# Rates, decays, operands, pairs and keys of each half of the heads pinned behind single steps of the column GEMMs, key copies on ACT

## The chip, the cores and the metric

The kernel runs on one core of a Trainium2 chip. The metric is the device time of one execution in microseconds (us).

## The reference

Two layers, each a half-step SwiGLU FFN, two token mixers side by side, and another half-step FFN; 256 tokens of 1024 numbers, all in fp32. The part around the change is the second mixer, RWKV-7:

```
p_b = token_shift_mix(p[..., GATE_WIDTH + 2 * A_WIDTH:], mu)      # p = h @ w_in
r, k, v = p[..., :B_WIDTH], p[..., B_WIDTH:2*B_WIDTH], p[..., 2*B_WIDTH:3*B_WIDTH]
log_w = -softplus(-(w0 + tanh(w_down) @ w2)) - 0.5
decay = exp(-exp(log_w))
a = sigmoid(a0 + a_down @ a2)
if v_first is not None:                                            # layer 1 only
    v = v + (v_first - v) * sigmoid(v0 + v_res_down @ v2)
kk = heads(k * k_k)
kk = kk / maximum(sqrt(sum(kk * kk, axis=-1)), 1e-12)
k = k * (1 + (a - 1) * k_a)
def step(state, inp):                                              # over the tokens
    sa = einsum('bhvk,bhk->bhv', state, kk_t)
    state = state * w_t - sa * (kk_t * a_t) + v_t * k_t
    return state, einsum('bhvk,bhk->bhv', state, r_t)
```

The first mixer (gMLP) needs `u` and `v` columns of the same `p`, a layer norm and a causal 128x128 product.

## The kernel before

**The GEMMs.** All large products run in fp32r with a high and a low part of each operand, three matmuls for one (`mm3` and the three lines of `chunk_b`). Weights come by DMA from SP's queue in units of 512 KB; each unit is cast on ACT (L220, high part) and subtracted on DVE (L221, low part), four units ahead of their use. ACT and DVE thus have a standing duty per unit beside whatever else they do.

**The columns of the second mixer.** k, r and v of each half of the heads (g = 0, 1; four column blocks of 128 each) are chunks of 96 matmuls of 128x256 (`chunk_b`), four steps of 24, one weight unit each. Behind a chunk `shift` mixes each block with the token before it: ACT L533, then DVE L534.

**What is made of them, per half g.** `rwkv_rates`: squares of k on ACT (L630), head sums on PE (L633), their inverse roots on DVE and POOL (L636, L637), spread on ACT (L642); the LoRA products of decay and a (L648, L661) with tanh on ACT (L650, L663) and one DVE pass (L651); in layer 1 also the mix of v with the first layer's (L674). `rwkv_pairs`, per pair of blocks q = 0, 1: cumulative decays (L702, exponentials on ACT L704 and L705), the spread norms turned by PE (L714) and multiplied with k (L716), the operands KR and bk on DVE (L721 to L733), 16 rows of small matmuls (L741, 32 in all), their masks on DVE (L744), and six transposes of bk (L752), copied out on DVE (L753). `rwkv_values`: v through a 128x128 matrix (L769) and r against k (L779).

**Behind the columns.** In `mixers` the second half of the gMLP's v and its u (chunks of 48 matmuls of 128x512, `chunk_a`), the gMLP's product (L520), then `rwkv_inverse`: 62 short DVE steps one after the other (L804, L806) and tiny matmuls (L817, L827); the values of half 1; `rwkv_chain` over four blocks of tokens with `rwkv_out` (L945); the gates and projections, whose GEMMs (L236 to L238) fill PE between the pieces of inverse and chain.

**The order.** Each engine runs its own instructions in order. A scheduler places them ahead of time, by priorities that follow the order of the code; so a chunk of GEMMs that the code writes later may be placed between the pieces of an earlier part. `issue_after` adds an edge to PE's order alone.

Of the kernel before, what the change touches and what calls it, by code (L numbers as in the profile page):

```python
# [16 lines left out]
P = 128  # L17
# [19 lines left out]
class Trunk:  # L37
# [196 lines left out]
    def mm3(self, ps, xh, xl, wh, wl, first, last):  # L234
        mm = self.nc.tensor.matmul
        mm(ps, lhsT=xh, rhs=wh, start=first, stop=False)  # L236
        mm(ps, lhsT=xh, rhs=wl, start=False, stop=False)  # L237
        mm(ps, lhsT=xl, rhs=wh, start=False, stop=last)  # L238
# [28 lines left out]
    def chunk_b(self, x):  # L267

        xh, xl = x
        ps = [self.gp().rearrange("p (i t) -> p i t", i=2) for _ in range(2)]  # L270
        mm = self.nc.tensor.matmul
        for i in range(4):
            hi, lo = self.take()
            for b in range(4):
                cs = slice(b * P, b * P + P)
                o = ps[b // 2][:, b % 2, :]
                for k in range(2):
                    kt = 2 * i + k
                    mm(o, lhsT=hi[:, k, cs], rhs=xh[kt // 4][:, kt % 4, :], start=(kt == 0 and b % 2 == 0), stop=False,  # L279
                       skip_group_check=True)  # L280
                    mm(o, lhsT=hi[:, k, cs], rhs=xl[kt // 4][:, kt % 4, :], start=False, stop=False, skip_group_check=True)  # L281
                    mm(o, lhsT=lo[:, k, cs], rhs=xh[kt // 4][:, kt % 4, :], start=False, stop=kt == NK - 1,  # L282
                       skip_group_check=True)
        return ps
# [323 lines left out]
    def rwkv_cols(self, l, ht, j, g):  # L608
        ps = self.chunk_b(ht)
# [3 lines left out]
        return o  # L613

    def rwkv_rates(self, l, g, st, gr):
# [4 lines left out]
        k_, v_ = gr["k"], gr["v"]  # L620
# [33 lines left out]
        for q in range(2):  # L654
            hp0 = 4 * g + 2 * q

            ps = self.mp().rearrange("p (i t) -> p i t", i=2)
            at = self.tt([P, 2, 256])
            for i in range(2):
                hs = slice((2 * q + i) * P, (2 * q + i) * P + P)  # L660
                mm(ps[:, i, :], lhsT=hi[:, 1, hs], rhs=xs[:, 1, :], start=True, stop=False)  # L661
                mm(ps[:, i, :], lhsT=lo[:, 1, hs], rhs=xs[:, 1, :], start=False, stop=True)
                nc.scalar.activation(at[:, i, :], ps[:, i, :], AF.Tanh, scale=0.5,  # L663
                                     bias=V[:, V_A0 + hp0 + i:V_A0 + hp0 + i + 1])
            gr["at"].append(at)
        for q in range(2 if l else 0):
# [15 lines left out]
        if l == 0 and self.depth > 1:  # L682
            nc.gpsimd.dma_start(self.vspill[g], v_)

    def rwkv_pairs(self, l, g, st, gr):
# [4 lines left out]
        TTm = nc.vector.tensor_tensor  # L690
        c8 = lambda t: t.rearrange("p i (c s) -> p (i c) s", s=64)
        jb, jk = g, 1 - g
        for q in range(2):
            hp0 = 4 * g + 2 * q
            k2, r2 = (gr[n][:, 2 * q:2 * q + 2, :] for n in ("k", "r"))
            at = gr["at"][q]

# [10 lines left out]

            rx = gr["rx"][q]
            kk = self.tt([P, 2, 256])  # L710
            ps = self.mp().rearrange("p (i t) -> p i t", i=2)
            for i in range(2):
                for tb in range(NTB):
                    nc.tensor.transpose(ps[:, i, tb * P:tb * P + P],  # L714
                                        rx[:, tb, 2 * i:2 * i + 2, :].rearrange("p h c -> p (h c)"), self.ident)
                nc.vector.scalar_tensor_tensor(kk[:, i, :], k2[:, i, :], V[:, V_KK + hp0 + i:V_KK + hp0 + i + 1],  # L716
                                               ps[:, i, :], ALU.mult, ALU.mult)
            KR = self.wt([P, 2, 4, 2, 64])
            KR8 = KR.rearrange("p i c j s -> p (i c) j s")
            nc.gpsimd.tensor_copy(KR8[:, :, 0, 0:1], c8(kk)[:, :, 0:1])  # L720
            TTm(KR8[:, :, 0, 1:64], c8(kk)[:, :, 1:64], c8(E)[:, :, 0:63], ALU.mult)  # L721
            TTm(KR8[:, :, 1, :], c8(r2), c8(E), ALU.mult)

            bk = self.wt([P, 2, 4, 2, 64])
            bk8 = bk.rearrange("p i c j s -> p (i c) j s")
            nc.vector.scalar_tensor_tensor(kk, at, 1.0, kk, ALU.add, ALU.mult)
            nc.vector.scalar_tensor_tensor(bk8[:, :, jb, :], c8(kk), -0.5, c8(Ei), ALU.mult, ALU.mult)
            for i in range(2):
                c = hp0 + i
                nc.scalar.activation(at[:, i, :], at[:, i, :], AF.Identity, bias=self.omka[l][:, c:c + 1],  # L730
                                     scale=self.hka[l][:, c:c + 1])
            TTm(at, at, k2, ALU.mult)
            TTm(bk8[:, :, jk, :], c8(at), c8(Ei), ALU.mult)  # L733

            for i in range(2):
                G = self.wt([P, 8, P])
                ps2 = [self.mp().rearrange("p (u t) -> p u t", t=P) for _ in range(2)]
                for c in range(4):
                    for par in range(2):
                        rs = slice(64 * par, 64 * par + 64)  # L740
                        mm(ps2[par][:, c, :], lhsT=bk[rs, i, c, :, :].rearrange("p j s -> p (j s)"),  # L741
                           rhs=KR[rs, i, c, :, :].rearrange("p j s -> p (j s)"), start=True, stop=True)
                for par in range(2):
                    TTm(G[:, 4 * par:4 * par + 4, :], ps2[par],  # L744
                        self.mask.rearrange("p (o t) -> p o t", o=1).broadcast_to([P, 4, P]), ALU.mult)
                gr["G"].append(G)

            BK = self.zp.tile([P, 2, 3, P], F32, tag="bk", name=self.nm("bk"), bufs=4)
            for i in range(2):
                ps = self.mp().rearrange("p (c k) -> p c k", k=P)  # L750
                for c in range(3):
                    nc.tensor.transpose(ps[:, c, :], bk[:, i, c, :, :].rearrange("p j s -> p (j s)"), self.ident)  # L752
# [204 lines left out]
    def mixers(self, l, ht, before, after):  # L957
        nc = self.nc
        sg, rw = {}, {}
        grs = [dict(KR=[], BK=[], VS=[], G=[]) for _ in range(2)]  # L960
# [17 lines left out]
        self.rwkv_values(l, 1, grs[1])  # L978
# [121 lines left out]
```

## Time and profile before

| | |
|---|---|
| median of 3 timed runs | 1452.43 us (1452.08 to 1455.58) |
| the profiled execution's own time | 1453.21 us |
| its span in the trace | 1451.5 us |
| busy: PE, DVE, ACT, POOL | 1380.1, 890.0, 745.5, 139.7 us |
| granted clock of PE, mean over the span | 0.984 |

The span is the stretch between first and last instruction that the profile shows; some 1.7 us of the time lie around it. Positions in the trace are microseconds from the span's start. The column stage of layer 0 lies at about 215 to 363 and that of layer 1 at about 927 to 1080.

### The profile page before, as it was taken

Reading aid. Unit: us, or ns where it says so; the run is one execution under the profiler, and the core shown is the slowest. Engines: PE = TensorE matmul, PEld = TensorE weight load, DVE = VectorE, ACT = ScalarE, POOL = GpSimd, SP = SyncE. Lnnn points to the kernel's source line nnn. Section 1 sums busy time; section 2 is a strip of 40 time slices with the busy share of each in tenths; the row PEclk is TensorE's granted clock in tenths of the full one; section 3 lists DMA queues with packets and bytes.
Section 4 is the critical chain, followed back from the end, with each engine's and each line's share of the span. In section 5 each row is a group of like instructions: output and inputs, shape, how many; then the busy total and the mean of one; then the engine's idle time right before and its main releaser. Section 6 shows DMA issues by size and latency. Waiting matters only on the chain. (4 is left out here: it accounts for less than half of the span.)

```text
span 1451.5 us, 21801 instructions
## 1 busy us (share of the span) xinstructions
PE 1380.1 (95%) x8642; PEld 1156.6 (80%) x8642; DVE 890.0 (61%) x1200; ACT 745.5 (51%) x1049; POOL 139.7 (10%) x200
## 2 busy tenths in 40 slices
PE   6999999999998999999999999999989999999996
PEld 5888879887777778888888888899867777788885
DVE  4555466778953565555555554769789536555553
ACT  5444456647464545444454443765564645545442
POOL 5000011114102100000010000110140011100000
PEclk9999999999989999999999999999999899999998
DMA  7765557444542567655575555674435325665552
GB/s 228 238 188 187 182 171 242 135 144 132 165 128 73 189 203 236 188 184 182 186 260 189 187 180 186 200 218 138 144 104 158 122 77 192 223 209 181 191 185 87
DMA packets 116871, 254.63 MB, mean 175 GB/s; under 512 B 8879, under 2 KB 12097, under 8 KB 116769
## 3 DMA queue, kind: packets, MB, share of 16 engines
q1 hardware_dynamic: 108048, 226.00, 48.6%
q0 software_dynamic: 8576, 26.72, 5.4%
q8 instruction: 68, 1.11, 0.3%
q10 hardware_dynamic: 144, 0.52, 0.1%
q14 instruction: 35, 0.28, 0.1%
HBM read 243.77 MB, written 9.44 MB: 174 GB/s over the span
## 5 line engine op out<-in xcount | busy, mean ns | idle before, releaser
L221 DVE TENSOR_TENSOR wl<-wr,wh 128x1024 fp32r<-128x1024 f32 x427 | 523.5, 1229 | 398.2 <-ACT wh L220 393.1
L220 ACT CAST wh<-wr 128x1024 fp32r<-128x1024 f32 x427 | 448.4, 1052 | 499.2 <-PE g L238 381.3
L236 PE MATMUL g<-wh,z 128*128 128x512 f32 x1088 | 430.3, 395 | 5.4 <-DVE z L985 2.9
L238 PE MATMUL g<-wh,z 128*128 128x512 f32 x1088 | 429.7, 395 | 3.0 <-DVE z L308 3.0
L237 PE MATMUL g<-wl,z 128*128 128x512 f32 x1088 | 428.8, 394 | 0.6 <-DVE wl L221 0.6
L236 PEld LDWEIGHTS g<-wh,z 128*128 128x128 f32 x1088 | 205.2, 189 | 48.8 <-ACT z L307 4.2
L238 PEld LDWEIGHTS g<-wh,z 128*128 128x128 f32 x1088 | 205.3, 189 | 48.1 <-DVE z L308 6.1
L237 PEld LDWEIGHTS g<-wl,z 128*128 128x128 f32 x1088 | 205.6, 189 | 42.8 <-DVE wl L221 1.8
L236 PE MATMUL g<-wh,w 128*128 128x512 f32 x416 | 162.8, 391 | 0.0
L238 PE MATMUL g<-wh,w 128*128 128x512 f32 x416 | 162.2, 390 | 0.0
L237 PE MATMUL g<-wl,w 128*128 128x512 f32 x416 | 162.2, 390 | 0.0
L281 PE MATMUL g<-z,wh 128*128 128x256 f32 x384 | 110.5, 288 | 0.0
L282 PE MATMUL g<-z,wl 128*128 128x256 f32 x384 | 110.2, 287 | 0.0
L279 PE MATMUL g<-z,wh 128*128 128x256 f32 x384 | 109.7, 286 | 0.0
L238 PEld LDWEIGHTS g<-wh,w 128*128 128x128 f32 x416 | 78.1, 188 | 16.2
L236 PEld LDWEIGHTS g<-wh,w 128*128 128x128 f32 x416 | 78.1, 188 | 15.8
L237 PEld LDWEIGHTS g<-wl,w 128*128 128x128 f32 x416 | 78.1, 188 | 15.7
L282 PEld LDWEIGHTS g<-z,wl 128*128 128x128 f32 x384 | 74.6, 194 | 0.5 <-issue 0.5
L281 PEld LDWEIGHTS g<-z,wh 128*128 128x128 f32 x384 | 74.7, 195 | 0.2 <-issue 0.2
L279 PEld LDWEIGHTS g<-z,wh 128*128 128x128 f32 x384 | 74.6, 194 | 0.2 <-issue 0.2
L457 POOL DMA_DIRECT2D xspill<-w x10 | 5.8, 578 | 634.5 <-DVE w L441 634.5
L303 PE MATMUL m<-ident,z 128*128 128x128 f32 x336 | 50.3, 277 | 14.3 <-DVE z L329 8.4
(228 smaller groups left out, 1249.8 us busy)
## 6 DMA issues: line engine op xcount, KB each, us to landing
wr<-in_ffn_w_gu_dram SPq DMA_DIRECT2D x176, 512.0 KB, 3.7
wr<-in_ffn_w_down_dram SPq DMA_DIRECT2D x88, 512.0 KB, 3.5
wr<-in_w_in_rest_dram SPq DMA_DIRECT2D x58, 512.0 KB, 3.5
wr<-in_w_in_first_dram SPq DMA_DIRECT2D x57, 512.0 KB, 3.7
wr<-in_w_proj_a_dram SPq DMA_DIRECT2D x16, 512.0 KB, 3.6
wr<-in_w_proj_b_dram SPq DMA_DIRECT2D x16, 512.0 KB, 3.6
wr<-in_w_out_dram SPq DMA_DIRECT2D x16, 512.0 KB, 4.4
xspill<-w POOLq DMA_DIRECT2D x10, 512.0 KB, 3.7
```

The lines of the kernel that those rows point to most:

```text
L220: nc.scalar.copy(hi, raw)
L221: nc.vector.tensor_tensor(lo, raw, hi.bitcast(F32), ALU.subtract)
L236: mm(ps, lhsT=xh, rhs=wh, start=first, stop=False)
L237: mm(ps, lhsT=xh, rhs=wl, start=False, stop=False)
L238: mm(ps, lhsT=xl, rhs=wh, start=False, stop=last)
L279: mm(o, lhsT=hi[:, k, cs], rhs=xh[kt // 4][:, kt % 4, :], start=(kt == 0 and b % 2 == 0), stop=False, skip_group_check=True)
L281: mm(o, lhsT=hi[:, k, cs], rhs=xl[kt // 4][:, kt % 4, :], start=False, stop=False, skip_group_check=True)
L282: mm(o, lhsT=lo[:, k, cs], rhs=xh[kt // 4][:, kt % 4, :], start=False, stop=kt == NK - 1, skip_group_check=True)
L303: nc.tensor.transpose(ps[:, i * P:(i + 1) * P], src[:, i * P:(i + 1) * P], self.ident)
L457: self.nc.gpsimd.dma_start(self.xsrc[tb], self.x[tb])
```

## The change

`rwkv_rates`, `rwkv_pairs` and the mix of v are cut into `rwkv_rates`, `rwkv_decays`, `rwkv_operands`, `rwkv_pairs`, `rwkv_keys` and `rwkv_vmix`. The column GEMMs, now generators (`cols_steps`, `chunk_steps`), are driven one step at a time; after a stated number of steps a part is written, with an order edge on PE behind the last matmul of that step. Rates no longer follow k, r and v of their half, but the fifth step (four of k, one of r). The second half's values, and the 512-wide v chunk, are part of the same run of steps. The copies of the transposed keys go from DVE to ACT.

```
     def rwkv_keys(self, q, gr):
...
             for c in range(3):
                 nc.tensor.transpose(ps[:, c, :], bk[:, i, c, :, :].rearrange("p j s -> p (j s)"), self.ident)
-                nc.vector.tensor_copy(BK[:, i, :, :], ps[:, 0:3, :])
+            nc.scalar.copy(BK[:, i, :, :], ps[:, 0:3, :])
...
+        def then(n, *parts):
+            for _ in range(n):
+                next(cols, None)
+            with self.tc.issue_after(self.last_mm):
+                for f in parts:
+                    f()
+
+        chunks = [self.rwkv_cols(l, ht, j, g, grs[g], n) for g in range(2) for j, n in ((1, "k"), (0, "r"), (2, "v"))]
+        cols = itertools.chain(*chunks, v1())
+        then(5)
         for g in range(2):
-            for j, n in ((1, "k"), (0, "r"), (2, "v")):
-                grs[g][n] = self.rwkv_cols(l, ht, j, g)
-            self.rwkv_rates(l, g, rw, grs[g])
-            self.rwkv_pairs(l, g, rw, grs[g])
+            gr = grs[g]
+            then(0, lambda: self.rwkv_rates(l, g, rw, gr))
+            then(2, lambda: self.rwkv_decays(l, g, rw, gr))
+            then(3, lambda: self.rwkv_operands(l, g, 0, gr), lambda: self.rwkv_operands(l, g, 1, gr))
+            then(1, lambda: self.rwkv_pairs(0, gr))
+            then(1, lambda: self.rwkv_pairs(1, gr))
+            then(1, lambda: self.rwkv_keys(0, gr), lambda: self.rwkv_keys(1, gr))
+            then(1, lambda: self.rwkv_vmix(l, g, rw, gr))
+            self.spill_values(l, g, gr)
+            then(1, lambda: self.rwkv_values(l, g, gr))
             if g == 0:
-                self.rwkv_values(l, 0, grs[0])
-        self.sgu_v_half(sg, 1, self.chunk_a(ht, False))
+                then(2)
+        for _ in cols:
+            pass
+        self.sgu_v_half(sg, 1, done[0])
...
         with self.tc.high_priority(offset=0):
             self.rwkv_inverse(grs)
-        self.rwkv_values(l, 1, grs[1])
```

Lines of the changed program: L295 to L298 are the column GEMMs, L221 and L222 cast and subtraction, L550 and L551 the shift, L647 to L659 the squares and norms, L665 to L680 the rates, L723 to L739 the decays, L756 to L768 the operands, L782 the pairs, L797 the keys, L813 and L823 the values, L861 the first tiny matmul of the inverse (L817 before).

**Where the head norms stand on PE.** Before, in layer 0, the head sums (L633) follow the last matmul of v (tile names: `g` a GEMM's PSUM tile, `m` a small one, `t` the squares):

```order
L279 MATMUL g_2085<-z_1588,wh_2047 128x256
L281 MATMUL g_2085<-z_1590,wh_2047 128x256
L282 MATMUL g_2085<-z_1588,wl_2048 128x256
L633 MATMUL m_2215<-blk_424,t_2216 128x2 x4
L633 MATMUL m_2215<-blk_424,t_2223 128x2 x4
L648 MATMUL m_2240<-w_1791,w_1779 128x512
```

In the changed program they (L650) stand among the matmuls of r, 66 GEMM rows behind k's last one:

```order
L295 MATMUL g_1954<-z_1588,wh_1886 128x256
L297 MATMUL g_1954<-z_1590,wh_1886 128x256
L298 MATMUL g_1954<-z_1588,wl_1887 128x256
L650 MATMUL m_1985<-blk_424,t_1986 128x2 x2
L665 MATMUL m_2010<-w_1791,w_1779 128x512
L666 MATMUL m_2010<-w_1792,w_1779 128x512
L650 MATMUL m_1985<-blk_424,t_1986 128x2 x2
```

The head sums have moved forward by the rest of r and all of v, from 192 GEMM rows behind k's end to 66.

**What DVE does ahead of the first pairs.** Before, in layer 0, first half, the last operands of q = 0 (to L733 into `w_2289`) with what stood around them, and the masks (L744) behind; `wl` is the low part of a weight unit:

```order
L726 SCALAR_TENSOR_TENSOR t_2277<-t_2251,t_2277 128x512
L221 TENSOR_TENSOR wl_2492<-wr_2429,wh_2491 128x1024
L727 SCALAR_TENSOR_TENSOR w_2289<-t_2277,t_2273 128x8x64
L732 TENSOR_TENSOR t_2251<-t_2251,w_1944 128x512
L534 SCALAR_TENSOR_TENSOR z_2549<-g_2427,vec_450,z_2549 128x255
L221 TENSOR_TENSOR wl_2522<-wr_2459,wh_2521 128x1024
L733 TENSOR_TENSOR w_2289<-t_2251,t_2273 128x8x64
L534 SCALAR_TENSOR_TENSOR z_2549<-g_2427,vec_450,z_2549 128x255
L776 SCALAR_TENSOR_TENSOR t_2251<-w_2075,vec_450,t_2251 128x256 x2
L221 TENSOR_TENSOR wl_2563<-wr_2489,wh_2562 128x1024
L744 TENSOR_TENSOR w_2296<-m_2297,mask 128x512
L744 TENSOR_TENSOR w_2296<-m_2298,mask 128x512
```

In the changed program the rows up to the last operand of q = 0 (L768 into `w_2237`); right ahead of them stand a subtraction (L222), the four products with the norms (L739) and two shifts of r (L551):

```order
L222 TENSOR_TENSOR wl_2176<-wr_2066,wh_2175 128x1024
L551 SCALAR_TENSOR_TENSOR w_2162<-g_1953,vec_450,w_2162 128x255
L551 SCALAR_TENSOR_TENSOR w_2162<-g_1954,vec_450,w_2162 128x255
L756 TENSOR_TENSOR w_2233<-t_2117,t_2101 128x8x63
L222 TENSOR_TENSOR wl_2206<-wr_2132,wh_2205 128x1024
L757 TENSOR_TENSOR w_2233<-w_2162,t_2101 128x8x64
L761 SCALAR_TENSOR_TENSOR t_2117<-t_2021,t_2117 128x512
L762 SCALAR_TENSOR_TENSOR w_2237<-t_2117,t_2102 128x8x64
L222 TENSOR_TENSOR wl_2258<-wr_2173,wh_2257 128x1024
L767 TENSOR_TENSOR t_2021<-t_2021,w_1944 128x512
L756 TENSOR_TENSOR w_2244<-t_2125,t_2111 128x8x63
L768 TENSOR_TENSOR w_2237<-t_2021,t_2102 128x8x64
```

The operands have moved from among the shifts of the other half's k (into `z`) to among those of r of their own half, and the operands of q = 1 (`w_2244`) begin before the masks of q = 0.

**The values of the second half on PE.** Before, in layer 0, they (L769, L779) stand among the tiny matmuls of the inverse (L827) and the first ones of the chain (L860):

```order
L827 MATMUL m_3574<-w_3347,w_3366 32x32
L827 MATMUL m_3575<-w_3347,w_3366 32x32
L238 MATMUL g_4393<-wh_4356,z_3314 128x512
L769 MATMUL m_3643<-cent,z_2811 128x128 x4
L779 MATMUL m_3652<-t_2864,blk_424 128x512
L860 MATMUL m_3660<-w_2399,w_2296 64x64
```

In the changed program they (L813, L823) stand in the 512-wide v chunk:

```order
L239 MATMUL g_2982<-wh_2862,z_1590 128x512
L813 MATMUL m_3061<-cent,z_2972 128x128 x4
L823 MATMUL m_3070<-t_2626,blk_424 128x512
L813 MATMUL m_3075<-cent,z_2972 128x128 x4
L823 MATMUL m_3084<-t_2634,blk_424 128x512
L237 MATMUL g_2981<-wh_2918,z_1588 128x512
```

They have moved from behind the inverse to a place ahead of it.

## Rows read from the trace of the kernel before

**Rows 1.** The page's first part: engine, busy us, share of the span, instructions.

```profile
PE 1380.1 (95%) x8642; PEld 1156.6 (80%) x8642; DVE 890.0 (61%) x1200; ACT 745.5 (51%) x1049; POOL 139.7 (10%) x200
```

**Rows 2.** Windows: stretch, length, then busy of PE, PEld, DVE, ACT, POOL, clock, DMA.

```profile
225.00:250.00 25.00, 25.00 (x211) 25.00 (x210) 17.56 (x22) 18.63 (x29) 4.22 (x8) 1.00 0.75 235
255.00:363.00 108.00, 100.30 (x720) 88.73 (x719) 81.68 (x130) 65.21 (x102) 26.30 (x24) 0.98 0.44 136
275.00:300.00 25.00, 23.41 (x210) 20.92 (x209) 24.65 (x41) 10.38 (x18) 1.48 (x3) 1.00 0.35 106
363.00:416.00 53.00, 47.73 (x269) 39.03 (x269) 50.56 (x103) 25.23 (x32) 4.65 (x9) 1.00 0.55 172
416.00:440.00 24.00, 24.00 (x431) 18.33 (x428) 6.62 (x10) 16.37 (x35) 2.65 (x4) 0.72 0.25 79
965.00:1080.00 115.00, 103.65 (x741) 91.82 (x739) 94.66 (x143) 63.94 (x105) 26.60 (x26) 0.98 0.46 144
```

**Rows 3.** Waits of PE in the column stages (255:363, then 965:1080): total, times, longest.

```profile
PE m L702 <- DVE w L651: 3.5, 2, 1.9
...
PE m L752 <- DVE w L744: 4.5, 4, 2.3
```

**Rows 4.** Timeline of PE and ACT at the head norms, layers 0 and 1.

```profile
255.27 0.39 PE L633 MATMUL m<-blk,t 128*128 128x2 f32 x3
...
242.48 1.30 ACT L630 ACTIVATE t<-w,vec 128x256 f32<-128x256 f32 x3
...
966.37 0.62 PE L633 MATMUL m<-blk,t 128*128 128x2 f32 x5
...
951.82 0.91 ACT L630 ACTIVATE t<-w,vec 128x256 f32<-128x256 f32 x2
```

**Rows 5.** Groups of POOL (215:363) and ACT (255:363): busy, mean ns, idle before.

```profile
L637 POOL TENSOR_TENSOR rn<-rn,mhalf 128x16 f32<-128x16 f32 x2 | 5.9, 2930 | 29.8 <-DVE rn L636 29.8
...
L220 ACT CAST wh<-wr 128x1024 fp32r<-128x1024 f32 x23 | 24.1, 1048 | 21.6 <-PE g L281 9.8 <-issue 6.4 <-PE g L238 4.3
...
L663 ACT ACTIVATE t<-m,vec 128x256 f32<-128x256 f32 x8 | 3.5, 477 | 0.5 <-PE m L662 0.5
...
L482 ACT ACT_TABLE_LOAD x2 | 2.6, 1283 | 0.0
...
L482 ACT ACTIVATE z<-g 128x512 f32<-128x512 f32 x2 | 1.2, 598 | 0.0
```

**Rows 6.** Groups of DVE in 255:363: busy, mean ns, idle before and its releasers.

```profile
L221 DVE TENSOR_TENSOR wl<-wr,wh 128x1024 fp32r<-128x1024 f32 x24 | 29.6, 1234 | 11.1 <-ACT wh L220 9.8 <-PE g L282 1.3
...
L753 DVE COPY bk<-m 128x384 f32<-128x384 f32 x8 | 4.0, 545 | 0.0
...
L733 DVE TENSOR_TENSOR w<-t,t 128x512 f32<-128x512 f32 x4 | 2.7, 687 | 0.1
...
L716 DVE SCALAR_TENSOR_TENSOR t<-w,vec,m 128x256 f32<-128x256 f32 x4 | 1.9, 477 | 0.1
```

**Rows 7.** Waits of PE after the column stages: 363:416, 1080:1143, 416:485, 1143:1215.

```profile
PE m L520 <- ACT ld L471: 2.0, 1, 2.0
...
PE g L236 <- DVE z L985: 1.3, 1, 1.3
PE m L817 <- DVE w L809: 0.5, 1, 0.5
...
PE g L236 <- DVE z L985: 1.6, 1, 1.6
...
PE m L945 <- DVE t L941: 7.1, 4, 1.8
...
PE m L945 <- DVE t L941: 6.3, 4, 2.3
```

**Rows 8.** Windows of the value matmuls L769 alone, first and second half of heads.

```profile
290.00:310.00 20.00, 2.21 (x16) 2.02 (x16) 1.00 0.47 140
415.00:440.00 25.00, 3.99 (x16) 3.73 (x16) 0.73 0.27 88
```

More of the change, by code (lines that the diff above doesn't have):

```diff
@@ L1 @@
+import itertools
 import math
@@ L237, in mm3 @@
         mm(ps, lhsT=xh, rhs=wl, start=False, stop=False)
-        mm(ps, lhsT=xl, rhs=wh, start=False, stop=last)
+        self.last_mm = mm(ps, lhsT=xl, rhs=wh, start=False, stop=last).ins
     def chunk_a(self, x, token_first):
@@ L265, in chunk_a, with chunk_steps, cols_steps @@
         return ps
-    def chunk_b(self, x):
+    def chunk_steps(self, x):
+        xh, xl = x
+        ps = [self.gp() for _ in range(NTB)]
+        for i in range(4):
+            hi, lo = self.take()
+            for tb in range(NTB):
+                ts = slice(tb * P, tb * P + P)
+                for k in range(2):
+                    kt = 2 * i + k
+                    self.mm3(ps[tb], xh[kt // 4][:, kt % 4, ts], xl[kt // 4][:, kt % 4, ts], hi[:, k, :], lo[:, k, :],
+                             kt == 0, kt == NK - 1)
+            yield
+        return ps
+    def cols_steps(self, x):
         xh, xl = x
@@ L281, in chunk_b @@
                     mm(o, lhsT=hi[:, k, cs], rhs=xl[kt // 4][:, kt % 4, :], start=False, stop=False, skip_group_check=True)
-                    mm(o, lhsT=lo[:, k, cs], rhs=xh[kt // 4][:, kt % 4, :], start=False, stop=kt == NK - 1,
-                       skip_group_check=True)
+                    self.last_mm = mm(o, lhsT=lo[:, k, cs], rhs=xh[kt // 4][:, kt % 4, :], start=False,
+                                      stop=kt == NK - 1, skip_group_check=True).ins
+            yield
         return ps
@@ L606, in rwkv_tail, with rwkv_cols @@
         st["ec"] = self.st([P, 8, 4], "ec", 1)
-    def rwkv_cols(self, l, ht, j, g):
-        ps = self.chunk_b(ht)
+    def rwkv_cols(self, l, ht, j, g, gr, name):
+        ps = yield from self.cols_steps(ht)
         o = (self.zt if g else self.wt)([P, 4, 256])
@@ L665, in rwkv_rates, with spill_values, rwkv_vmix @@
             gr["at"].append(at)
+    def spill_values(self, l, g, gr):
+        if l == 0 and self.depth > 1:
+            self.nc.gpsimd.dma_start(self.vspill[g], gr["v"])
+    def rwkv_vmix(self, l, g, st, gr):
+        nc = self.nc
+        V = self.vec[l]
+        mm = nc.tensor.matmul
+        TTm = nc.vector.tensor_tensor
+        v_, hv, xs = gr["v"], st["lw"][g][2], st["xs"]
         for q in range(2 if l else 0):
@@ L681, in rwkv_rates, with rwkv_decays @@
             nc.vector.scalar_tensor_tensor(v2, d, 0.5, v2, ALU.mult, ALU.add)
[L682 to L685 removed]
+    def rwkv_decays(self, l, g, st, gr):
         nc = self.nc
@@ L707, in rwkv_pairs @@
                                   E.rearrange("p i (c s) -> p i c s", s=64)[:, :, :, 63])
-            rx = gr["rx"][q]
+            gr["E"].append((E, Ei))
+        for q in range(2):
+            hp0 = 4 * g + 2 * q
+            ps = self.mp().rearrange("p (i t) -> p i t", i=2)
             kk = self.tt([P, 2, 256])
-            ps = self.mp().rearrange("p (i t) -> p i t", i=2)
             for i in range(2):
@@ L748, in rwkv_pairs @@
[L748 to L752, printed above, removed]
-                nc.vector.tensor_copy(BK[:, i, :, :], ps[:, 0:3, :])
-            gr["KR"].append(KR)
-            gr["BK"].append(BK)
+                                        gr["rx"][q][:, tb, 2 * i:2 * i + 2, :].rearrange("p h c -> p (h c)"), self.ident)
@@ new lines, in rwkv_pairs @@
+    def rwkv_pairs(self, q, gr):
+        nc = self.nc
+        KR, bk = gr["KR"][q], gr["bk"][q]
+        for i in range(2):
+            G = self.wt([P, 8, P])
+            ps2 = [self.mp().rearrange("p (u t) -> p u t", t=P) for _ in range(2)]
+            for c in range(4):
+                for par in range(2):
+                    rs = slice(64 * par, 64 * par + 64)
+                    nc.tensor.matmul(ps2[par][:, c, :], lhsT=bk[rs, i, c, :, :].rearrange("p j s -> p (j s)"),
+                                     rhs=KR[rs, i, c, :, :].rearrange("p j s -> p (j s)"), start=True, stop=True)
+            for par in range(2):
+                nc.vector.tensor_tensor(G[:, 4 * par:4 * par + 4, :], ps2[par],
+                                        self.mask.rearrange("p (o t) -> p o t", o=1).broadcast_to([P, 4, P]), ALU.mult)
+            gr["G"].append(G)
@@ L757, in rwkv_values, with rwkv_keys @@
+    def rwkv_keys(self, q, gr):
+        nc = self.nc
+        bk = gr["bk"][q]
+        BK = self.zp.tile([P, 2, 3, P], F32, tag="bk", name=self.nm("bk"), bufs=4)
+        for i in range(2):
+            ps = self.mp().rearrange("p (c k) -> p c k", k=P)
+            for c in range(3):
+                nc.tensor.transpose(ps[:, c, :], bk[:, i, c, :, :].rearrange("p j s -> p (j s)"), self.ident)
+            nc.scalar.copy(BK[:, i, :, :], ps[:, 0:3, :])
+        gr["BK"].append(BK)
     def rwkv_values(self, l, g, gr):
```

72 lines of the change are left out of this document (36 added, 36 removed).

## The prediction

> **What bounds the kernel now.** The page comes first: PE is busy for 1380.1 of 1451.5 us [rows 1], so only what keeps PE waiting, or slow, can be won. The windows by stage come second, to see where that is [rows 2]. A stretch of plain column GEMMs (225 to 250) has PE busy throughout: 211 matmuls in 25.00, or 0.1185 us each, 2.84 for a step of 24. Where rates and pairs lie, in 255 to 363 and 965 to 1080, PE is busy for 100.30 of 108 and 103.65 of 115: 7.7 and 11.35 us of waiting. The clock, 0.98 there on the mean, takes another 108 x 0.02 = 2.2 and 2.3. That pool, 23.5 us, is what the change can reach directly. The waits come third, to see for whom PE waits [rows 3]: in layer 0 3.5 us, in two stops of up to 1.9, for DVE's pass behind the decay's tanh (L651); in layer 1 4.5 us, up to 2.3, for the masks on DVE (L744). DVE is no innocent there: in 275 to 300 it is busy for 24.65 of 25 [rows 2]. So the stage has two limits in turn, a chain of short steps over four engines right behind v, and then DVE's throughput.
>
> **The change part by part.** *Cost of the parts themselves.* The matmuls, exponentials and operands are the same. The key copies, 8 of 545 ns in each layer [rows 6], leave DVE, 4.4 us per layer where it is full. On ACT the trace has no such copy; the nearest rows take 477 ns for 256 columns and 598 for 512 out of PSUM [rows 5], so some 0.55 for 384, between these two. ACT is busy for 10.4 of 25 us in 275 to 300 [rows 2], so I take nothing for it; were that cover gone, 4.4 us would go back on the path of the casts.
>
> *Head norms.* The old stops at L702 go, since the norm sums no longer stand behind v. But in their new place PE comes for them early. In layer 0, v ends at 255.27 [rows 4]; two chunks earlier (192 x 0.1185 = 22.75) k ended, at 232.5; 66 GEMMs on, PE reaches L650 at 240.3. The squares of k began on ACT at 242.48 and take 0.43 each [rows 4], and nothing in the change brings them forward, for ACT is held up by the arrival of the LoRA weights ahead of k's shift. The first is there at 242.9: **2.6 us of new waiting**. In layer 1 the same count (966.37 - 22.75 = 943.6, and in its order 44 GEMMs on, 948.8) meets squares ready at 951.82 + 0.45 = 952.3: **3.5 us**.
>
> *First pairs, first half of layer 0.* The four squares with a cast among them end the norm sums at about 244.6; the root on POOL takes 2.93 [rows 5], so 247.7. ACT then has four spreads (no dearer than a tanh, 0.48), a cast (1.05), four tanh (1.9), a table load (1.28), an exponential (0.60) and the next cast [rows 5]: 7.8 us, 255.5. DVE's order then wants the subtraction that waits for that cast and three more (4 x 1.23 = 4.9), four products with the norms and four shifts (8 x 0.48 = 3.8) and seven operand passes (7 x 0.69 = 4.8) [rows 6] before the first pairs can start: 13.5, at 269.0. PE has 139 GEMMs (16.5) and some 28 small matmuls between, which the trace of this stage lets me put at 4 to 7 us; it arrives at 263.4 to 266.4. I take 266, since small ones keep being slower than their count: **3.0** of waiting (up to 5.6). The second pairs have behind them a subtraction and eight passes of DVE, 6.7 us, against two steps' remainder and the first pairs on PE, 4.1: **2.6**. So this half costs 8.2.
>
> *The other halves.* Counted alike: in layer 1's first half 3.5 + 2.2 + 2.9 = 8.6. The second halves have k in time, since no late weights stand ahead of it, and keep only the DVE debt of the pairs: 4.4 in layer 0, 4.5 in layer 1. All four make 25.7, against a pool of 23.5 that goes: **+2.2**. If operands come a step (2.84) earlier or later at each of the eight pairs, but not below nothing, this is -15 to +20; nearer to the middle, because the rows of DVE are known and only the pieces of PE between are guessed. A fall of the clock behind a new stop I cost at nothing: it delays PE's arrival at the next stop, which is set by DVE, and that stop gets shorter.
>
> *Values of the second half.* They leave the stretch 416 to 440, where the clock is 0.72 [rows 2]: L769 is busy there for 3.99 us and at full clock for 2.21 [rows 8], 1.8 too much, with L779 (as much again, an estimate) 3.6 a layer. But the slow stretch may simply take in other matmuls. Between 0 and 7.2 for both layers I take **-3.0**.
>
> *Behind the columns.* In the new order the projection no longer stands right behind L985's release of PSUM: the stops of 1.3 and 1.6 go [rows 7], **-2.9**; the wait of 2.0 for the transposed gMLP weights (L471) falls to about 0.5, **-1.5**. The inverse is DVE's alone, busy for 50.56 of 53 in 363 to 416 [rows 2], and as long as before, about 48 us; the scheduler has put 27 fewer 512-wide GEMMs (some 0.24 each, two of 256) ahead of its first matmul in layer 0, so PE comes there about 6.5 us earlier, DVE only some 3 earlier: a stop of 3 in place of 0.5 [rows 7], and I take 1 for layer 1: **+3.5**. The GEMMs left over (in layer 1 some 45, 10 us) fill stops at L945, 7.1 and 6.3 us [rows 7]; these wait on chains that the GEMMs can only partly cover: **-3.0**, between 0 and -8.
>
> *Sum.* 1453.2 + 2.2 - 3.0 - 2.9 - 1.5 + 3.5 - 3.0 = 1448.5, for the profiled execution, which took 0.8 more than the median. Against the median I forecast **1447.7, say 1448 us**: stops in the columns traded for others, a few us from behind them.
>
> [...] The trace shows a gelu with 0.0 us of idle time behind its table load of 1283 ns [rows 5]. [...]
>
> **The rivals.** *The pins hide everything.* If the matmuls between the pins take PE longer than I count and DVE, with 4.4 us of copies gone per layer, is in time, the 23.5 go and only half of 25.7 comes: 1448 - 13 = about 1435. For it speaks that DVE is full only in parts of the stage (81.68 of 108 [rows 2]); against it that its idle time there is mostly waiting for casts (9.8 of 11.1 before L221 [rows 6]), behind which the operands queue.
>
> *Slower: the operands queue behind the casts.* DVE runs in order, so a subtraction whose cast is late on ACT holds the operands behind it. If that happens before each of the eight pairs for one step, the stops grow by 8 x 1.2 = 10, to about 1458; it decides once the last operand of a first pair comes later than about 4.5 us behind PE. [...]
>
> *The inverse takes it all back.* DVE's 48 us bound what lies behind: if PE merely waits longer at L861 and the fillers find no gaps, the -3.0, -2.9 and -1.5 are lost: 1453 to 1456.
>
> **How the numbers follow.** A measurement of this kernel can tell about 0.3% (4.4 us) from no change: faster is below 1448.1, slower above 1456.8. Forecast (1442 to 1455), 0.45: the bound cuts through it, 0.20 faster, 0.24 the same, 0.01 slower. Everything hidden (1428 to 1442), 0.22: faster. Operands late or clock low (1454 to 1468), 0.20: 0.02 the same, 0.18 slower. The inverse takes it back, 0.13: 0.01 faster, 0.07 the same, 0.05 slower. Together 0.43, 0.33, 0.24. The range, 1434 to 1461, leaves out the far half of the second and third case.
>
> **What would show it.** Right: in the columns of layer 0 PE stops of 2 to 4 us at L650 (for ACT's squares) and L782 (for DVE's L768) and none at L723; idle time there of 12 to 14 in the first layer; a stop of 2 to 4 at L861; L813 in the v chunk at full clock; DVE free of key copies. Wrong: no stop at L650, which would mean that ACT's squares came forward, or a stop at the pins above 5 us; or, behind the columns, a shorter inverse.

## The result: 18 us slower, and the profile after

The changed kernel takes 1470.64 us (median of 4, 1465.88 to 1473.75) against 1452.91 us: ratio 1.0123, interval 1.0107 to 1.0138. The forecast was 1448, in a range up to 1461. The profiled execution took 1473.43 us, its span 1471.7 us, 20.2 us more than before.

The time is not in the stops. The first line of the page shows it, beside [rows 1]:

```profile
PE 1396.6 (95%) x8642; PEld 1176.5 (80%) x8642; DVE 881.6 (60%) x1184; ACT 748.2 (51%) x1061; POOL 128.0 (9%) x200
```

PE runs the same 8642 matmuls as before, but is busy with them for 16.5 us longer; its waiting (span less busy time) went from 71.4 to 75.1 us, only 3.7 more. These are PE's waits in the column stage of layer 0 (215 to 366), then those of layer 1 (915 to 1095) and of the stretch behind it (1095 to 1240), in the columns of [rows 3]:

```profile
PE m L678 <- ACT t L680: 4.8, 2, 2.7
PE m L650 <- ACT t L647: 3.0, 1, 3.0
PE m L782 <- DVE w L768: 1.3, 1, 1.3
PE m L782 <- DVE w L785: 0.5, 1, 0.5
...
PE m L650 <- ACT t L647: 3.5, 1, 3.5
PE m L678 <- ACT t L680: 3.2, 2, 2.2
PE m L782 <- DVE w L768: 2.2, 2, 1.2
PE m L782 <- DVE w L785: 1.1, 2, 0.5
...
PE m L487 <- POOL ld L481: 8.0, 1, 8.0
PE m L989 <- DVE t L985: 4.6, 3, 2.0
PE m L861 <- DVE w L853: 1.3, 1, 1.3
```

The stops of before at the decays and the masks [rows 3] are gone, and so are those of the first pairs for their last operand, here in the kernel before, layers 0 and 1:

```profile
PE m L741 <- DVE w L733: 0.9, 1, 0.9
...
PE m L741 <- DVE w L733: 2.4, 1, 2.4
```

New ones of about the same sum have come: 9.6 us in layer 0, where before had 7.3, and 10.0 in layer 1, where before had 11.0. One stop was in no forecast: 8.0 us at the transposes of the gMLP's mixing weights (L487). The windows show the rest (columns of [rows 2]):

```profile
234.00:245.30 11.30, 8.31 (x69) 8.11 (x68) 7.16 (x9) 8.08 (x13) 1.11 (x2) 1.00 0.76 248
245.30:252.20 6.90, 6.90 (x31) 6.57 (x31) 1.02 (x4) 1.59 (x3) 1.39 (x1) 0.51 0.41 140
...
958.70:969.00 10.30, 8.77 (x37) 8.38 (x38) 4.94 (x9) 4.91 (x10) 1.96 (x2) 0.50 0.47 163
...
996.00:1003.00 7.00, 6.46 (x32) 6.25 (x32) 4.85 (x10) 1.09 (x2) 0.00 (x0) 0.52 0.25 77
...
1096.50:1109.00 12.50, 4.51 (x16) 3.94 (x17) 9.74 (x20) 4.25 (x6) 6.03 (x6) 0.59 0.76 222
...
1152.00:1171.00 19.00, 18.87 (x364) 15.88 (x365) 2.41 (x3) 14.10 (x29) 0.00 (x0) 0.55 0.19 58
```

The reader should look at the clock, third from the right. Right behind the stop at the head sums PE is fully busy (6.90 of 6.90), but at a granted clock of 0.51 (0.50 in each half microsecond from 245.5 to 252.0, 1.00 from 252.5 on), and with 31 matmuls where plain columns have 58 (211 in 25.00 [rows 2]). The same holds at the 3.5 us stop in layer 1 (0.50 from 958.7 on; the stop ends at 960.2) and behind the inverse (0.55 from 1152 on). At the 8.0 us stop (1096.5) more than half of the low stretch falls into the stop itself, where PE has nothing to run: 0.50 from 1099 to 1108, and PE idle until 1104.5. Length of stop alone does not decide it: among the pairs of layer 1 (996) the low stretch comes behind stops of only 1.2 and 0.5 us, and behind the 2.0 us stop at L678 in layer 0 the clock stays at 1.00 from 252 to 310. As one figure, an estimate from span and clock: span x (1 - mean clock) is what the lower clock can cost at most, 1451.5 x 0.016 = 23.2 us before and 1471.7 x 0.029 = 42.7 now. The difference, 19.5, is nearly the whole 20.2, and near the 16.5 us that PE is busy longer. At most 8.5 of it, half of 6.8 and 10.2 us, lies right behind the two stops at the head sums; the rest is spread over the columns and what follows them. The four executions agree with one another on it: 1473.4 and 1473.8 us at a mean clock of 0.971, 1467.9 at 0.973, 1465.9 at 0.976.

What PE ran behind the first stop is seen in its timeline, changed kernel, from the head sums on (some rows left out, among them all GEMMs):

```profile
244.56 0.61 PE L650 MATMUL m<-blk,t 128*128 128x2 f32 x4 [2.99 <-ACT t L647]
...
245.76 0.85 PE L650 MATMUL m<-blk,t 128*128 128x2 f32 x4
...
249.60 0.85 PE L650 MATMUL m<-blk,t 128*128 128x2 f32 x4
251.31 2.36 PE L723 MATMUL m<-tri,w 128*128 128x128 f32 x16
256.51 0.39 PE L678 MATMUL m<-w,w 128*128 128x256 f32 x1 [2.02 <-ACT t L680]
```

and its second stop on ACT and POOL:

```profile
250.81 2.98 POOL L654 TENSOR_TENSOR rn<-rn,mhalf 128x16 f32<-128x16 f32 x1 [9.62 <-DVE rn L653]
...
253.82 0.40 ACT L659 COPY t<-rn 128x256 f32<-128x256 f32 x1 [5.51 <-POOL rn L654]
254.13 1.04 ACT L221 CAST wh<-wr 128x1024 fp32r<-128x1024 f32 x1
255.08 1.01 ACT L659 COPY t<-rn 128x256 f32<-128x256 f32 x3
255.99 0.82 ACT L680 ACTIVATE t<-m,vec 128x256 f32<-128x256 f32 x2
```

ACT stands for 5.51 us in front of the spreads, for the root on POOL; a cast and the tanh that frees PSUM for L678 are queued behind it. That the head sums end only at 250.5, at a clock of 0.51, makes this wait longer.

### The profile page after: what moved, and what is told of

Read it like the earlier page. It is cut to its first block, busy times and chain, and to the rows that moved or that the text cites. A ratio compares the mean times of both kernels' runs of the same rounds, so it can differ in the third digit from the quotient of the medians.

```text
span 1471.7 us, 21808 instructions
## 1 busy us (share of the span) xinstructions
PE 1396.6 (95%) x8642; PEld 1176.5 (80%) x8642; DVE 881.6 (60%) x1184; ACT 748.2 (51%) x1061; POOL 128.0 (9%) x200
## 4 chain that ended last, share of the span: by engine, by line
PE 74%; DVE 10%; ACT 5%; DMA 4%; issue 3%; POOL 2%; POOLq 0%; ACTq 0%; SPq 0%; DVEq 0%
PE g L239 19%; PE g L238 19%; PE g L237 19%; DVE wl L222 5%; ACT wh L221 3%; PE m L320 2%; PE g L297 2%; PE g L298 2%; PE g L295 2%; DMA wr<-in_w_in_first_dram 1%; DVE w L850 1%; POOL rn L654 1%; PE m L924 1%; ACT w L837 1%; DMA wr<-in_w_in_rest_dram 1%
## 5 line engine op out<-in xcount | busy, mean ns | idle before, releaser
L222 DVE TENSOR_TENSOR wl<-wr,wh 128x1024 fp32r<-128x1024 f32 x427 | 523.6, 1229 | 429.6 <-ACT wh L221 425.8
L221 ACT CAST wh<-wr 128x1024 fp32r<-128x1024 f32 x427 | 448.6, 1052 | 509.0 <-PE g L239 386.6
L295 PE MATMUL g<-z,wh 128*128 128x256 f32 x384 | 111.7, 291 | 0.0
L298 PE MATMUL g<-z,wl 128*128 128x256 f32 x384 | 111.3, 290 | 0.0
L295 PEld LDWEIGHTS g<-z,wh 128*128 128x128 f32 x384 | 75.4, 196 | 0.8 <-issue 0.5
L298 PEld LDWEIGHTS g<-z,wl 128*128 128x128 f32 x384 | 75.6, 197 | 0.2 <-issue 0.2
```

Source lines behind the costliest of these rows:

```text
L221: nc.scalar.copy(hi, raw)
L222: nc.vector.tensor_tensor(lo, raw, hi.bitcast(F32), ALU.subtract)
L298: self.last_mm = mm(o, lhsT=lo[:, k, cs], rhs=xh[kt // 4][:, kt % 4, :], start=False, stop=kt == NK - 1, skip_group_check=True).ins
```

## The experiments

Theory A: the loss is the stop at pins whose operands are late, above all at the head sums, together with the low clock behind it. Rival B: the small matmuls, packed among the GEMMs, lower the clock wherever they stand. C: behind the columns DVE's inverse bounds the time, so stops won there come back. All ratios are to the kernel before, with 95% intervals. A "low stretch" below is a stretch of the trace in which the granted clock is about half (0.50 to 0.52 in the windows above that lie within one).

| run | median us | ratio | mean clock of the profiled run |
|---|---|---|---|
| e1, all pins of the half later | 1454.03 | 1.0018 (1.0001 to 1.0035) | 0.979 |
| e2, mixing weights early | 1478.34 | 1.0175 (1.0160 to 1.0190) | 0.966 |
| e3, e1 and e2 | 1458.02 | 1.0041 (1.0026 to 1.0056) | 0.979 |
| e4, only the rates moved | 1461.61 | 1.0061 (1.0044 to 1.0078) | 0.978 |
| e5, e1 and mixing weights in mid columns | 1454.87 | 1.0018 (1.0008 to 1.0028) | 0.977 |
| e6, e1 and tanh ahead of spreads | 1453.55 | 1.0012 (0.9999 to 1.0025) | 0.980 |
| e7, key copies on ACT alone | 1456.15 | 1.0034 (1.0021 to 1.0047) | 0.984 |
| e8, e5 and e6 | 1451.17 | 1.0004 (0.9987 to 1.0021) | 0.975 |
| e9, e1 and values back | 1457.73 | 1.0035 (1.0022 to 1.0048) | 0.979 |
| e10, values alone moved | 1458.18 | 1.0044 (1.0030 to 1.0059) | 0.982 |
| e11, e6 and v's second chunk early | 1454.62 | 1.0013 (0.9998 to 1.0029) | 0.978 |
| e12, e11 and values back | 1451.63 | 1.0001 (0.9989 to 1.0014) | 0.984 |
| e13, e4 with later rates | 1453.62 | 1.0013 (1.0004 to 1.0022) | 0.983 |
| e14, changed kernel, LoRA weights early | 1457.07 | 1.0038 (1.0022 to 1.0053) | 0.975 |
| e15, e12 and LoRA weights early | 1447.21 | 0.9965 (0.9953 to 0.9977) | 0.983 |

**e1: later pins.** The first number of steps sets where the rates of the first half stand, and with them every later part of that half: all of it moves back by three steps, and the second half by one. Below this is called "later rates".

```
-        then(5)
+        then(8)
...
-                then(2)
+                then(0)
```

> The changed kernel with the first half's rates pinned behind the eighth step instead of the fifth (and the second half's behind the eighteenth instead of the seventeenth). Theory A (the loss is the low clock behind stops at pins whose operands are late): the stops of 3.0 and 3.5 us at L650 go, and with them the low clock of 6.8 and 10.2 us behind them (3.4 and 5.1 us lost); the time falls by 12 to 15 us against the changed kernel, to about 1456 to 1459, and the mean clock rises from 0.971 to about 0.977. Rival B (small matmuls packed among the GEMMs lower the clock wherever they stand, stop or no stop): only the two stops go, 6.5 us, about 1464, the clock stays at 0.971 to 0.973.

16.6 us less than the changed kernel: no stop at L650 in either layer, and in the windows of 232 to 244 and 244 to 254 the clock is 1.00 and 0.83, where the changed kernel has its low stretch:

```profile
232.00:244.00 12.00, 12.00 (x103) 12.00 (x102) 7.25 (x9) 8.55 (x14) 1.12 (x2) 1.00 0.84 263
244.00:254.00 10.00, 8.95 (x57) 8.48 (x57) 3.88 (x6) 7.00 (x16) 2.93 (x1) 0.83 0.57 176
```

As A had it, a little beyond its range. By the profiles PE waits 9.2 us less than in the changed kernel and is busy 10.3 us less. But the edit moves all small matmuls of the half as well as it takes the stop away, so B is not yet out; and the low stretch that is left in layer 0, 3.4 us from 246.5 on, comes behind no stop of 1 us or more.

**e14: the head sums nearly in place, their operands ready.** The second half's LoRA weights go into tiles of their own, so that ACT is not held ahead of k's shift; the pin is set so that the head sums stand 6 PE rows later than in the changed kernel in layer 0 (28 in layer 1). The other parts of the first half move too: the decays stand 52 rows later in both layers.

```
-            raw, raw2 = self.ld([P, 2, 512]), self.ld([P, 2, 512])
+            alloc = self.zt if g else self.ld
+            raw, raw2 = alloc([P, 2, 512]), alloc([P, 2, 512])
...
-        then(5)
+        then(7)
...
-                then(2)
+                then(0)
```

> The changed kernel with the second half's LoRA weights loaded into tiles of their own, early enough that ACT is not held ahead of the shift of k, and the head sums kept at nearly their place on PE by a pin behind the seventh step (layer 0: row 1055 where the changed kernel has them at 1049; the second half's pins as there). The small matmuls stand among the same GEMMs; only what they wait for is ready. Theory A: no stop at the head sums, no low clock behind them, 12 to 17 us less than the changed kernel, 1453 to 1459. Rival B (density, not the stop): only the stops go, 6.5 us, and the clock stays near 0.971 to 0.973, about 1464.

13.6 us less, as A expected; B's 1464 is missed. By the profiles PE waits 8.3 us less than in the changed kernel and is busy 7.7 us less. No stop at the head sums is left. A stop of 3.3 us at the next place (L679, L678 before this edit's extra line, for the tanh behind the spreads) remains in both layers, with far less behind it, as these two windows of layers 0 and 1 show:

```profile
244.00:256.00 12.00, 8.68 (x61) 8.48 (x60) 3.83 (x7) 7.45 (x17) 1.94 (x1) 0.86 0.36 119
...
958.00:969.00 11.00, 10.08 (x73) 10.08 (x74) 5.93 (x10) 8.52 (x17) 0.71 (x1) 0.84 0.24 66
```

**e4 and e13: the rates alone moved, at two pins.** All else of each half stands behind v as before the change, the values of the second half behind the inverse; the key copies stay on ACT. e4 keeps the fifth step, e13 differs by the pin alone.

```
             then(0, lambda: self.rwkv_rates(l, g, rw, gr))
+            for _ in range(7):        # e13: 4, after then(8)
+                next(cols)
+            last = self.last_mm
+            next(cols)
+            with self.tc.issue_after(last):
+                self.rwkv_vmix(l, g, rw, gr)
+                self.rwkv_decays(l, g, rw, gr)
+                for q in range(2):
+                    self.rwkv_operands(l, g, q, gr)
+                    self.rwkv_pairs(q, gr)
+                    self.rwkv_keys(q, gr)
```

> One part of the change alone: the rates behind the fifth and seventeenth step, all the rest of each half behind v as before the change (key copies on ACT, values of the second half behind the inverse). Theory A: the stops at L650 with their low clock are there (15 us over both layers), the stops behind v for the decay's tanh are not (about 10 us with their clock), so 3 to 8 us more than the kernel before, about 1456 to 1460. Rival B: the small matmuls are spread over more GEMMs than in the changed kernel, so the clock is as before, and the time within 3 us of the kernel before.

> The kernel with only the rates moved (e4), but the first half's rates behind the eighth step and the second half's behind the twentieth. Theory A (stop at L650 and low clock behind it): the stops of 2.9 and 3.05 us and the low stretches of 6.8 and 10.2 us go, 8 to 14 us less than e4's 1461.6, about 1448 to 1453. Rival B (the rates' small matmuls among the columns lower the clock wherever they stand): within 4 us of e4, 1458 to 1464.

e4 has the stops at L650 (2.9 and 3.05 us) and is 8.9 us above before, a little more than A's 3 to 8; e13 is 8.0 below e4, at the near edge of A's range and outside B's. The windows behind the head sums, e4 first, then e13, layers 0 and 1:

```profile
245.00:253.00 8.00, 8.00 (x41) 7.76 (x41) 0.94 (x3) 1.97 (x5) 2.97 (x1) 0.57 0.35 120
...
959.00:969.00 10.00, 10.00 (x45) 9.61 (x45) 2.50 (x6) 3.98 (x9) 3.95 (x3) 0.50 0.51 145
```

```profile
245.00:253.00 8.00, 5.30 (x38) 4.82 (x39) 3.49 (x6) 5.00 (x13) 2.93 (x1) 1.00 0.66 205
...
959.00:969.00 10.00, 7.17 (x47) 6.88 (x46) 3.33 (x7) 7.12 (x15) 4.06 (x3) 0.83 0.63 213
```

e13 has waits of its own there (5.30 busy of 8), yet the clock holds. In layer 0 (215 to 340) the waits at L650 and L678, again e4 first:

```profile
PE m L650 <- ACT t L647: 2.9, 1, 2.9
PE m L678 <- ACT t L680: 2.7, 2, 1.4
```

```profile
PE m L678 <- ACT t L680: 4.5, 2, 2.4
...
PE m L650 <- ACT t L647: 0.3, 1, 0.3
```

Most of what leaves L650 comes back at L678, in layer 1 as well (3.0 and 1.3 in e4, 4.1 at L678 in e13). Over the whole span PE waits 71.2 us in e4 and 70.4 in e13, but it is busy for 1388.4 and 1381.2 us with the same matmuls. So the 8 us are the clock's: stops at the head sums are dear, stops of nearly the same sum at L678 cost far less. This and e14 speak against B, for the small matmuls of the rates stand among the columns in all of them. What in the stop at L650 sets off the low stretch, its length or the small matmuls right behind it, is not shown.

**e2, e3, e5: the 8 us stop at L487.** In e2 the mixing weights go into other tiles and ahead of v's norm; e5, on top of e1, reads and turns them behind the first half's second pairs.

```
-        ws = self.ld([P, 8, P])          # e5 keeps this line
+        ws = self.zt([P, 8, P])
...
-        wsT = self.ld([P, 8, P])
+        wsT = self.zt([P, 8, P])
...
-        self.sgu_v_norm(l, sg)
         sg["wsT"] = self.sgu_weights(l)  # e5: then(0, ...) behind pairs(1), g == 0
+        self.sgu_v_norm(l, sg)
```

> The changed kernel with the gMLP's mixing weights loaded into tiles of their own and before the norm of v, so that PE's transposes of them (L487) need not wait for POOL. Theory A: the stop of 8.0 us in layer 1 and the low clock of 10.2 us behind it go (5.1 us lost), and the stop of 1.15 in layer 0; 10 to 14 us less than the changed kernel, about 1457 to 1460. Rival C (what lies behind waits for DVE's inverse in any case): the time goes to L861, where PE then stops for as much longer; within 3 us of the changed kernel, about 1468 to 1471.

> Both edits of the two runs before. Theory A: the two gains add, 22 to 28 us, about 1443 to 1448, so below the kernel before, and the clock at 0.982 or more. Rivals B and C: 6 to 10 us less than the changed kernel, about 1461 to 1465.

> The kernel with the later rates (e1) and the gMLP's mixing weights read and turned behind the first half's second pairs instead of behind the columns. Theory A (stops cost themselves and the low clock behind them): the stops at L487 of 5.2 and 5.6 us and the low clock behind them (3.4 and 6.8 us long, 5.1 us lost) go, up to 16 us, at least 6: 1438 to 1448. Rival C (behind the columns DVE's inverse bounds the time): the stops reappear ahead of the inverse or at L861, and the time stays within 4 us of e1, 1450 to 1458.

e2 missed both: 7.7 us slower still. Its load is queued on POOL behind LoRA loads of the next layer (in layer 0 theirs are issued from 369.7 on, its own at 374.4), so in layer 0 the stop at L487 grew from 1.15 to 7.1, and in layer 1 3.3 of the 8.0 stayed. e3 carries the same fault (6.7 and 6.1 us at L487) and lies between its two expectations. e5 does remove the stops at L487, and the time stays that of e1, as C said: the next instruction takes the wait over, here PE's waits from 340 to 420:

```profile
PE m L320 <- DVE z L542: 6.4, 1, 6.4
PE m L861 <- DVE w L853: 1.4, 1, 1.4
```

L542 is the gMLP's product on DVE, behind v's norm and the first steps of the inverse on the same engine (in e8 the steps begin at 356.1, the product at 366.9).

**e6 and e8: the spreads off the tanh's path.** In the rates the LoRA products and their tanh are written ahead of the spreads; e8 is e5 with this.

```
-        gr["rx"] = ...  # four copies on ACT, moved behind the two loops below
         sg = self.wt([P, NTB, 512])
...
             gr["at"].append(at)
+        gr["rx"] = ...
```

> The kernel with the later rates (e1), with the LoRA products and their tanh written ahead of the spreads of the norms, so that ACT does not hold the tanh (L680) and a cast behind the root on POOL. Theory A: the stops at L678 (0.96, 0.93, 3.07 and 1.0 us) shrink to under 0.5 each, 4 to 6 us less than e1, about 1448 to 1450. Rival D (the spreads are on the path of the decays and operands, so that PE then waits at L736 or L782 instead): within 2 us of e1, 1452 to 1456.

> Later rates, mixing weights in mid columns and tanh ahead of spreads together. Theory A: the gains add, 1434 to 1444, faster than the kernel before by over 0.5%, mean clock 0.983 or more. Rivals C and D: 1448 to 1456, no faster than before.

In e6 the stops at L678 (now L673) shrink from 0.96, 0.93, 3.07 and 1.0 to 0.4 and 1.6 in all, but its time is e1's: D by the time, A by the stops. e8 has the fewest stops so far and is level with before; its twelve executions run from 1448.1 to 1461.0, with the mean clock: 1448.7 at 0.981, 1461.0 at 0.969. In its profiled execution (1455.8) PE waits 64.2 us, 7.2 less than before, and is busy 9.7 us longer: the lower clock takes back what the stops gave.

**e7: key copies on ACT alone**, on the kernel before.

```
-                nc.vector.tensor_copy(BK[:, i, :, :], ps[:, 0:3, :])
+                nc.scalar.copy(BK[:, i, :, :], ps[:, 0:3, :])
```

> The kernel before, with only the key copies moved from DVE to ACT. If DVE's load in the column stages bounds the stops there (the prediction's reading): 2 to 5 us faster than before, 1448 to 1451. Rival E (the stops wait for the chain over the engines, not for DVE's throughput): within 2 us of before.

0.34% slower, outside both expectations. The copy itself is cheap on ACT (480 ns, where DVE takes 545 [rows 6]); its mean clock is that of before (0.984), so the clock does not explain it. PE waits 73.3 us, 1.9 more than before, with 2.4 at L303 in layer 1 and 3.6 at L520 in layer 0 (2.0 before). Why is not settled.

**e9, e10, e12: the values of the second half.** e10 moves them alone, on the kernel before, ahead of the inverse; e9 and e12 put them back behind it, on e1 and on e11.

```
-            if g == 0:                                   # e10
-                self.rwkv_values(l, 0, grs[0])
+            self.rwkv_values(l, g, grs[g])
...
-        self.rwkv_values(l, 1, grs[1])
```

> The kernel before, with only the values of the second half moved from behind the inverse to behind the second half's pairs. The prediction's own term: 3 us faster (0 to 7), about 1449. Theory F: no gain or a loss of up to 5 us, 1452 to 1457, with a longer low stretch behind the inverse than 13.7 and 10.2 us.

> The kernel with the later rates (e1) and the values of the second half back behind the inverse, where the kernel before has them. The prediction's own term: 3 us slower than e1 (between 0 and 7), since the values then run at the lower clock again, about 1455 to 1458. Theory F (the values' long matmuls among the tiny ones keep the clock from staying low; without them the low stretch at inverse and chain of layer 1 grew from 10.2 to 17 and more): 3 to 7 us faster than e1, 1447 to 1451, with the low stretch behind the inverse under 14 us in both layers.

> e11 with the values of the second half behind the inverse. Theory F: 3 to 7 us less than e11. The prediction's term: 3 us more than e11.

e10 is 6 us slower than before: F's direction, beyond its range; the prediction's gain of 3 is not there. By the profiles PE is busy 5.7 us longer than before and waits 1.2 less. The stretch behind the inverse in layer 1, first in the kernel before, then in e10, each from the arrival at the inverse on:

```profile
1140.00:1164.00 24.00, 22.97 (x453) 17.87 (x452) 8.43 (x11) 17.92 (x36) 2.68 (x4) 0.79 0.27 90
```

```profile
1146.00:1170.00 24.00, 22.26 (x400) 18.08 (x401) 4.50 (x5) 18.37 (x36) 0.00 (x0) 0.64 0.21 66
```

Without the long matmuls of the values between the tiny ones the clock is lower there, 0.64 for 0.79: 24 x 0.15 = 3.6 us. But the kernel before has a further low stretch behind this window (3.4 us from 1175.5 on). Over 48 us from the arrival at the inverse on, the mean clock is:

| | layer 0 | layer 1 |
|---|---|---|
| before (values behind the inverse) | 0.86 | 0.86 |
| e10 (ahead of it) | 0.86 | 0.82 |
| e12 (behind) | 0.89 | 0.86 |
| e11 (ahead) | 0.68 | 0.86 |
| e9 (behind) | 0.86 | 0.86 |
| e1 (ahead) | 0.89 | 0.68 |

In each pair the clock is lower with the values ahead in one layer of the two, by 0.04 to 0.21, and the same or slightly higher in the other. The times follow it only in e10 for certain. e12 is 3.0 us below e11, but the executions of both spread over more than that (1448 to 1456, 1448 to 1459). e9 goes the other way, 3.7 us above e1, with intervals that overlap; it has a stop of 2.2 us at L702 that e1 has not, and longer ones at L487 (6.6 and 6.8 for 5.2 and 5.6). So the low clock is F's in part, and the time is not F's alone.

**e11: v's second chunk between the halves**, on e6; u's chunks follow the second half in the same run of steps.

```
-        cols = itertools.chain(*chunks, v1())
+        cols = itertools.chain(*chunks[:3], v1(), *chunks[3:], u())
...
-                then(0)
+                then(6)
```

> Later rates and tanh ahead of spreads (e6), and the second chunk of the gMLP's v between the two halves' columns instead of behind them, with u in the run of steps. Theory G (the stops of 5 to 8 us behind the columns come from v's late chunk: its norm on DVE and POOL is not done when u ends): no stop above 2 us at L488 (the transposes) or at the transposes of the gMLP's product; 6 to 12 us less than e6, 1442 to 1448. Rival C (DVE's inverse bounds what lies behind): the stops go to the inverse's first tiny matmul, and the time stays within 4 us of e6.

G nearly, by the stops: none at the transposes of the mixing weights, at most 2.4 at the gMLP's transposes. The time is e6's (1.1 us more), as C said, but not for C's reason: the stops did not go to the inverse's first tiny matmul (L862, 1.5 and 1.6). There is a low stretch of 20 us behind the first layer's inverse instead.

**e15: the version with what was learnt.** Later pins, tanh ahead of the spreads, v's chunk early, values back, LoRA weights early (the edits of e11, e9 and e14).

> The kernel of the last run before (v's second chunk early, later rates, tanh ahead of spreads, values back) with the LoRA weights early. If stops are what is left to win: 2 to 5 us less than its 1451.6, so 1447 to 1450, faster than the kernel before by 0.2 to 0.4%. Otherwise the same as it.

0.35% faster than before, by its interval, and as expected. Its column stages, in the windows of [rows 2]:

```profile
255.00:363.00 108.00, 98.84 (x726) 88.95 (x724) 86.06 (x130) 69.50 (x109) 23.13 (x27) 1.00 0.48 151
...
965.00:1080.00 115.00, 103.77 (x729) 92.69 (x729) 90.83 (x135) 71.42 (x116) 22.99 (x25) 0.96 0.45 140
```

PE waits there no less than before (9.2 and 11.2 us, 7.7 and 11.4 before): the stops only changed their names. In layer 0 the clock is full, in layer 1 a little lower. Over the whole span PE waits 4.0 us less than before and is busy as long (67.4 and 1379.6 us), so the gain is less waiting outside these two stretches.

## Why the prediction was wrong

**The step that failed** is the sentence "A fall of the clock behind a new stop I cost at nothing". The first stop was right: 2.6 and 3.5 us forecast at L650, 3.0 and 3.5 measured, on ACT's squares as said. The low stretches behind it, 6.8 and 10.2 us long, cost up to 3.4 and 5.1 and were not made up for by a shorter next stop: at a clock of 0.51 the head sums of layer 0 end at 250.5, where 244.6 was forecast, and the root, the spreads and the tanh behind them with them. In all, the mean clock is 0.97 in 215 to 366 and 0.94 in 915 to 1095, up to 15 us where the sum has nothing; the pool of 23.5, on the other side, had counted the old stops' lower clock (4.5) as won. e13 puts a price on the stops at L650 alone: 8.0 us, with PE waiting nearly as long in all as in e4. e1 and e14 give back 16.6 and 13.6 us, but move other parts too.

**A second step failed** behind the columns, the -1.5 for the mixing weights. The wait meant there went from 2.0 to 1.3 in layer 0; but v's second chunk had moved to the end of the run, its norm on DVE and POOL was late, and the load, which reuses the norm's tiles, later still (in layer 1 issued at 1097.7, before at 1068.1): stops of 1.1 and 8.0 us at L487. Removing them (e5) gave nothing, for the next instruction waits in their place; so what this step cost in time is open.

**The rival that came nearest** was the slower one, "Operands late or clock low", given 0.20 between 1454 and 1468. A low clock is what the trace shows: 0.51 and 0.50 at the stops at L650, for 6.8 and 10.2 us, up to 3.4 and 5.1 us of cost. Late operands at the pairs are hardly there, with 5.1 us of stops in all. What its range allows for a low clock at each stop no run shows; the runs show in its place the 8.0 us between e4 and e13, and no fixed price of a stop: in e13, with stops at L678 of up to 2.4 us in layer 0, the clock is 1.00 from 245 to 253. No case reached 1470.

**Stops at the pairs** were over-counted: in the first half of layer 0 3.0 forecast at the first pairs and none measured, 2.6 at the second and 1.8 (1.3 and 0.5); in all four halves 19.6 forecast and 5.1 measured. DVE was not early: it had the last operand of the first pairs at 273.0, not 269.0. But PE came at 273.2, not 266, held up by its stops and the clock. In place of these stops came those at L678, 4.8 and 3.2 us, which the count of ACT's queue had in view (four spreads ahead of the tanh) but only for the operands, not for PE. So the sum of the new stops, 25.7 forecast and 19.6 measured, came near by luck.

**Behind the columns**, the stops for L985 of the kernel before went, as forecast (-2.9); those at L945 (now L989) fell from 13.4 to 10.0, near the -3.0; L861 has 1.3 in each layer where 3 and 1 were said.

**Values, -3.0**: alone they cost 6 us (e10). **Key copies, nothing**: alone 0.34% (e7). Both had the work right and the time wrong. The parts do not add up: e13, which has the rates and the key copies moved, is within 0.2% of before.

**Open**: why e7 is slower, why the values' place has another sign in e9, and why some low stretches (at 996 in the changed kernel, at 246.5 in e1) follow short stops only. That a given order comes out up to 13 us apart from one execution to the next (e8) with the clock says that sums of this size are near the limit of what can be told apart here.

## What to carry to other kernels

A pin that brings PE to an instruction before its operand is there can cost more than the wait, as at L650 here (a stop of 3.0 us, then 6.9 us at 0.51): count the stretch at the lower clock behind it, and look which instructions PE has next, for here they were the rest of the head sums, which ended at 250.5, while POOL stood for 9.62 us ahead of the root and ACT for 5.51 ahead of the spreads. When work moves forward, move its operands' loads forward too, or leave room: here three steps were worth 8 us for the rates alone (e4 and e13), and 16.6 with the parts behind them (e1). Compare PE's busy time for the same matmuls, and not only its waits: in e4 and e13 (1388.4 and 1381.2 us busy, 71.2 and 70.4 us waiting) it told a loss to the clock from a loss to stops. Long matmuls between tiny ones are not only work; where they were taken away here, the clock of what stayed was lower in one layer of the two, by 0.04 to 0.21.

## What was unexpected of the hardware

Stops of 3.0 and 3.5 us at L650 came with 6.8 and 10.2 us at about half clock (0.51, 0.50 in the windows), the first right behind its stop, with PE busy throughout, the second from 1.5 us before its stop ends; stops of 3.3 us in e14 by less (0.86 and 0.84 over 12 and 11 us), and a stop of 2.4 us in e13 by none in layer 0. In the changed kernel PE runs 24 small matmuls and 6 of the columns' from 244.56 to 251.3, behind the stop at L650 (0.51), and 4 and 18 from 256.5 to 259.2, behind the 2.0 us stop at L678 (1.00); whether this makes the difference was not tried by itself. One program, run again, differs by up to 13 us (e8, 1448.1 to 1461.0), and its mean clock with it (0.981 at 1448.7, 0.969 at 1461.0).
